# A hybrid decoder layer on one core: recursion heads in two contiguous halves, output weights split later, 112 places per expert dealt over 16 groups of rows

## The chip, the cores and the metric

The kernel runs as one program on one core of a Trainium2 chip. The metric is the time of one execution in device microseconds. Of the kernel before there are three runs, 2958.97 to 2961.05 us, with a median of 2959.9 us. The profile of it is of a further execution, which took 2961.59 us; its trace spans 2959.8 us, and TensorE's mean granted clock in it is 0.96 of full speed.

The engines are called PE (TensorE), ACT (ScalarE), DVE (VectorE), POOL (GpSimd) and SP (SyncE, which here does little but issue transfers); a q behind the name (SPq) is the sequencer of that engine, which issues its transfers.

## The reference

One layer with 2048 tokens of 1024 numbers. Eight heads run a recursion over time, eight others an attention with forgetting; their outputs go through one output projection, and a mixture of 64 small experts follows, two per token.

```python
h = rms_norm(x, norm_mix_w)
p = h @ w_in
y_rw = rwkv7_mixer(p[..., :RW_COLS], ...)   # 8 heads of 64: S_t = S_{t-1} diag(w_t) + (S_{t-1} a_t) b_t^T + v_t k_t^T; y_t = S_t r_t
y_fox = fox_mixer(p[..., RW_COLS:], ...)    # 8 heads of 64: causal softmax attention, logits shifted by a running sum of log f
x = x + concatenate([y_rw, y_fox]) @ w_out
h = rms_norm(x, norm_ffn_w)
# hierarchical_moe: the best of 8 groups, in it the best 2 of 8 experts; gates from two softmaxes
y = sum over a token's 2 experts of gate * ((silu(h @ w_gate[e]) * (h @ w_up[e])) @ w_down[e])   # 1024 -> 512 -> 1024
x = x + y
```

With the reference's inputs the router gives an expert 64 tokens on average (4096 over 64 experts) and at most 101. Experts 0, 1 and 2 get 63, 52 and 30, the last two 50 and 79.

## The kernel before

**Stages.** The tokens are worked in 16 tiles (i) of 128. The projection of the recursion's heads fills the time to about 600 us, the attention's projection follows to about 850 us. Then attention and recursion run side by side to about 1430 us, the output projection, the norm, the router and the expert tables (`mix`) to about 1735 us, and the experts (`moe`) to the end. In every stage the order of the instructions on PE, ACT, DVE and POOL is written by a planner (`Lanes`): each piece of work is a generator which yields the engine and a modelled cost before its instructions, or the name of an event it waits for; `lanes.mark(name, delay)` sets an event. SP's transfers go into the program at the moment at which the planner reaches them, and SP issues them in that order; the planner gives them no cost.

**Recursion (`chain`).** Each tile is handled in 4 chunks (c) of 32 tokens. `gram2` and `gram3` have computed the chunk's small matrices before and written them to a tensor in DRAM per tile, `pkd`; the blocks of inverses lie in another, `TTd`. `load(i)` fetches a tile from there: AM (lines 1340 to 1342), TTb (line 1346), and for each of two kinds of heads (`e`, which lie in different halves of the partitions) the operands UV and SW (line 1357), YW (lines 1359 and 1362) and the decay `dec` (line 1364). Head h is here 2q + e: kind 0 holds the even heads and kind 1 the odd ones, so that in DRAM each kind is every other block of 64 columns. That is why line 1357 issues one transfer per chunk: 4 + 8 per kind, 24 per tile. A tile has 39 such loads, and `outputs` writes its result to `yd` in 8 transfers. A chunk makes `us` from UV on PE, copies it back into UV (ACT, line 1400), then makes the new state and the outputs Y; line 1380 is the first product of a tile with TTb.

**Output weights (`out_open`).** The two halves of `w_out` are loaded into `wst` (line 245, on SP) and each split into two fp16 parts: ACT makes the high part `wo` (line 255), DVE the low one (line 259). The first half's eight pieces are spread between the attention's work from the moment at which `out_open` starts.

**Tables (`mix`, `moe_table`).** For every token the router computes its two experts, its place in each (how many tokens chose it before), and the gate. POOL writes (token, gate) by an indirect transfer (line 1767) into row `place * 64 + expert` of one of two tables in DRAM, `tab[q]`. `moe_table` (line 1921) loads the first SL = 104 places of all experts into `tb`, place on partition: the first table by one transfer on POOL, the second by one on ACT. DVE then makes the index `idx` as the smaller of both (line 2008) and the gate as their sum. A place that no token took has an index beyond the last token, and a gather or a scatter skips it. Experts with more than SL tokens would get a second pass in a loop behind the stage, which with these inputs runs no time.

**Experts (`experts`).** Per expert: POOL gathers the token rows (line 2088, 4 KB each), PE transposes them (line 2104), the weights (gate, up, down; 2 MB each) come over SP into staging buffers `st` and are split into fp16 parts by ACT (line 1969) and DVE (line 1973), PE multiplies with gate and up (lines 2146 to 2148), `h` is made, transposed by PE in eight steps (line 2178) and copied to HT by ACT (line 2181), PE multiplies with down (lines 2139 to 2141), ACT scales by the gate (line 2196), and POOL adds the rows to the output by an indirect transfer (line 2202). In every product the places of the expert are the stationary side and 512 columns of weights stream. The staging buffers are dealt out by a list that is written by hand; from about the 33rd expert on all loads share four of them. In the planner a load costs 5.83 and a gather or a scatter 1.18 us of one common transfer queue ("Q").

Of the kernel before, what the change touches and what calls it, by code (L numbers as in the profile page):

```python
# [8 lines left out]
F32 = mybir.dt.float32  # L9
# [17 lines left out]
NG = 4  # L27
E = 64
DE = 512
SL = 104  # L30
NB = -(-T // SL)
CDEC = 0.5 * math.exp(-0.5)
WS = 64.0
# [69 lines left out]
class Kern:  # L103
# [453 lines left out]
    def rwkv_front(self):  # L557
# [8 lines left out]
        with ExitStack() as es:  # L566
# [223 lines left out]
            def gram2(i):  # L790

                s = St[i]
                A2, R2, BK = s["A2"], s["R2"], s["BK"]
                s["g1"] = g1 = smp.tile([128, 8, 2, 32], F32, name="g1", tag="sm")
                s["g2"] = g2 = smp.tile([128, 8, 2, 32], F32, name="g2", tag="sm")
                for h in range(8):
                    q, e = divmod(h, 2)
                    for c in range(4):
                        t = slice(32 * c, 32 * c + 32)
                        nc.tensor.matmul(g1[t, h], A2[:, e, q, t], BK[:, :, q, t], start=True, stop=True)  # L800
                for h in range(8):
                    q, e = divmod(h, 2)
                    for m in range(2):
                        for c in range(4):
                            t = slice(32 * c, 32 * c + 32)
                            nc.tensor.matmul(g2[t, h, m], BK[:, m, q, t], R2[:, e, q, t], start=True, stop=True)

            def gram3(i):
                s = St[i]
                g, j = divmod(i, 4)  # L810
                pk, g1, g2 = s["pk"], s["g1"], s["g2"]
                L = wk.tile([128, 8, 32], F32, name="L", tag="s0")
                ml = self.mlow[:, 0:1].to_broadcast([128, 8, 32])
                TT(L, g1[:, :, 0], ml)
                TT(s["AM"][:, :, 0:32], g1[:, :, 1], ml)
                for m, o in ((0, self.PK_QB), (1, self.PK_QK)):
                    TT(pk[:, o:o + 256].rearrange("p (e q t) -> p q e t", e=2, q=4),
                       g2[:, :, m].rearrange("p (q e) t -> p q e t", e=2),
                       self.mup[:, 0:1, None, :].to_broadcast([128, 4, 2, 32]))
# [489 lines left out]
    def chain(self, lanes, step_at, uwp, usp, yp):  # L1309
# [10 lines left out]
            yield "P", 0.9  # L1320
            nc.gpsimd.memset(t, 0.0)
        for s in range(2):
            t = self.pw.tile([128, 4, 8, 64], F32, name=f"UV{s}", tag=("l2", "l3")[s])
            yield "P", 1.8
            nc.gpsimd.memset(t, 0.0)
            UVs.append(t)
            t = (ch, self.pw)[s].tile([128, 32, 64], F32, name=f"SW{s}", tag=("SW", "h3")[s])
            yield "P", 1.9
            for e in range(2):
                r = slice(64 - 64 * e, 128 - 64 * e)  # L1330
                nc.gpsimd.tensor_scalar(t[r].rearrange("p (c e) d -> p c e d", e=2)[:, :, e],
                                        self.id32[r, None, r].to_broadcast([64, 16, 64]), 1.0, 0.0,
                                        op0=OP.mult, op1=OP.add)
            SWs.append(t.rearrange("p (c h) d -> p c h d", h=8))

        def load(i):
            s, pkd = St[i], self.pkd[i]
            g, j = divmod(i, 4)
            am, ma = AM.rearrange("p (q e) c -> p q e c", e=2), pkd[:, 0:768].rearrange("p (q e c) -> p q e c", q=4, e=2)
            nc.sync.dma_start(am[:, :, 0, 32:128], ma[:, :, 0])  # L1340
            nc.sync.dma_start(am[:, :, 1, 0:64], ma[:, :, 1, 32:96])
            nc.sync.dma_start(am[:, :, 1, 96:128], ma[:, :, 1, 0:32])
            for c in range(4):
                t = slice(32 * c, 32 * c + 32)
                o = (j * 4 + c) * 8
                nc.sync.dma_start(TTb[t, :, t], self.TTd[g][o:o + 8].rearrange("h (k i) -> k h i", k=32))
            ct = lambda o, n: pkd[:, o:o + n].rearrange("(c t) f -> t c f", c=4)
            s["YW"] = YW = ch.tile([128, 4, 2, 4, 32], F32, name="YW", bufs=2)
            s["dec"] = dec = ch.tile([128, 4, 4], F32, name="dec", bufs=2)
            for e in range(2):  # L1350
                u, st = 64 * e, slice(64 - 64 * e, 128 - 64 * e)
                hd = lambda x: x.rearrange("t c (q e d) -> t c q e d", e=2, d=64)[:, :, :, e]
                own = lambda x, r: x[r].rearrange("t c (q e) d -> t c q e d", e=2)[:, :, :, e]
                for x, m, o in ((UVs[i % 2], 1, self.PK_V), (SWs[i % 2], 0, self.PK_B), (SWs[i % 2], 1, self.PK_K)):
                    r = slice(u + 32 * m, u + 32 * m + 32)
                    for c in range(4):
                        nc.sync.dma_start(own(x, r)[:, c], hd(ct(o, 512))[:, c])
                for m, o in ((0, self.PK_QB), (1, self.PK_QK)):
                    nc.sync.dma_start(YW[u + 32 * m:u + 32 * m + 32, :, e].rearrange("p c q t -> p c (q t)"),
                                      ct(o + 128 * e, 128))  # L1360
                r = slice(u, u + 64)
                nc.sync.dma_start(YW[st, :, e].rearrange("p c q t -> p c (q t)"),
                                  pkd[r, self.PK_R:self.PK_R + 512].rearrange("p (c f) -> p c f", c=4))
                nc.sync.dma_start(dec[st].rearrange("p q c -> p (q c)"), pkd[r, self.PK_DEC:self.PK_DEC + 16])

        def prep(i):

# [18 lines left out]
        def chunk(i, c):  # L1386
# [1 line left out]
            yield f"t{step_at[8 * i + 2 * c]}"  # L1388
            yield "us"
            yield "T", 0.6  # L1390
            uv = UV[:, c].rearrange("p (q e) d -> p e q d", e=2)
            U = usp.tile([128, 4, 64], F32, name="us")
            for h in range(8):
                q, e = divmod(h, 2)
                nc.tensor.matmul(U[64 * e:64 * e + 32, q], UW[:, h, 32 * c:32 * c + 32], UV[:, c, h],
                                 start=True, stop=True)
            for e in range(2):
                yield "A", 0.32
                r = slice(64 * e, 64 * e + 32)
                nc.scalar.activation(uv[r, e], U[r], AF.Copy)  # L1400
            lanes.give("us")
            if c == 0:
                yield "Y"
# [1 line left out]
            if (i, c) != (NT - 1, 3):  # L1405
                yield "us"
                yield "T", 0.5
                S = usp.tile([128, 4, 64], F32, name="us")
                for h in range(8):
                    q, e = divmod(h, 2)  # L1410
                    nc.tensor.matmul(S[64 - 64 * e:128 - 64 * e, q], SW[:, c, h], UV[:, c, h], start=True, stop=True)
            lanes.start("y", outputs(i, c, UV))
            if (i, c) != (NT - 1, 3):
                nxt = UVs[i % 2][:, c + 1] if c < 3 else UVs[(i + 1) % 2][:, 0]
                nxt = nxt.rearrange("p (q e) d -> p e q d", e=2)
# [7 lines left out]
        def outputs(i, c, UV):  # L1423
            s = St[i]
            yield "T", 0.33
            for h in range(8):
                q, e = divmod(h, 2)
                r = 64 * e + 32 * (q % 2)
                nc.tensor.matmul(s["Y"][r:r + 32, c, q // 2], s["YW"][:, c, e, q], UV[:, c, h], start=True, stop=True)
            if c == 3:  # L1430
                yield "A", 0.48
                y = ch.tile([128, 4, 2, 64], F32, name="y", bufs=2)
                nc.scalar.activation(y, s["Y"], AF.Copy)
                yd = self.yd[i].rearrange("(c t) (p m e d) -> t m e c p d", c=4, p=2, m=2, e=2)
                for e in range(2):
                    for m in range(2):
                        r = 64 * e + 32 * m
                        for q in range(2):
                            nc.sync.dma_start(yd[:, m, e, :, q], y[r:r + 32, :, q])
                lanes.give("Y")  # L1440
                lanes.mark(f"tile{i}")

# [15 lines left out]
    def out_open(self):  # L1458
# [4 lines left out]
        wo = self.eo[0].tile([128, 2, KB, 512], F16, name="wo", tag="wo")  # L1463
        self.wo = [[wo[:, 0], wo[:, 1]]]
        split = self.split_block([w_out[:, :512]], None)
        yield from split.steps(*self.wo[0])
        yield "last"
        split = self.split_block([w_out[:, 512:]], None)
# [814 lines left out]
```

## Time and profile before

| | |
|---|---|
| median of 3 runs | 2959.9 us (2958.97 to 2961.05) |
| profiled execution, its span | 2961.59 us, 2959.8 us |
| PE busy | 2590.1 us (88%) |
| DVE busy | 2382.3 us (80%) |
| ACT busy | 1754.1 us (59%) |
| POOL busy | 814.1 us (28%) |
| transfers | 645.47 MB, mean 218 GB/s |

The profile divides the span into 40 equal slices of 74 us and gives the busy share of each engine per slice in tenths. PE's share of 88% is a mean over stages with different limits: it says little about what ends last in a stage. That is read from the waits, which name for each stretch of idle time the instruction that ended it, and from the timelines, in which each row has its start in us, its duration in us, the engine, the line of the kernel, the operation with its tiles, and in brackets the idle time before it with what ended it. In a window's row the busy time of PE, PE's weight loads, DVE, ACT and POOL stand in this order, each with its number of instructions, then PE's granted clock, the mean busy share of the 16 DMA engines and the GB/s that they moved.

### The profile page before, as it was taken

The page shows a single profiled execution, that of the slowest core. Times are in us where ns is not written, and L with a number is a line of the kernel's source. Part 1 is how long each engine was busy: PE and PEld are TensorE (multiplying, and loading weights), DVE is VectorE, ACT ScalarE, POOL GpSimd, SP SyncE. Part 2 cuts the span into 40 slices and gives each one's busy share as a digit, 9 for nine tenths or more (in the row PEclk, how much of TensorE's full clock was granted, in tenths as well). Part 3 has the DMA queues.
Part 4 walks back from the last instruction along what each step waited for, and adds up shares of the span by engine and source line. Part 5 has one row for each costly group of instructions (what it writes and reads, how often), then busy time and mean ns, then how long its engine had stood idle before and what let it go on. Part 6 is the DMA issues. An engine that isn't in the chain of part 4 may idle for free. (4 is left out here: it accounts for less than half of the span.)

```text
span 2959.8 us, 53150 instructions
## 1 busy us (share of the span) xinstructions
PE 2590.1 (88%) x20309; PEld 1442.4 (49%) x20309; DVE 2382.3 (80%) x4278; ACT 1754.1 (59%) x2470; POOL 814.1 (28%) x729
## 2 busy tenths in 40 slices
PE   4997888799998999989888859999999989999897
PEld 2554445345444555444344435555555555555554
DVE  6788898863565787868989879888889888888886
ACT  5544434422243555546344448888888778787786
POOL 2212111223033545435545431222221111111111
PEclk8999999899999999989998979999999999999999
DMA  5343434433244544432465369999999999999996
GB/s 175 126 160 110 139 136 151 154 115 91 91 122 105 124 94 120 90 89 76 155 225 170 136 221 349 361 361 349 359 346 360 337 357 359 356 357 363 361 364 210
DMA packets 313678, 645.47 MB, mean 218 GB/s; under 512 B 183850, under 2 KB 229152, under 8 KB 288077
## 3 DMA queue, kind: packets, MB, share of 16 engines
q1 hardware_dynamic: 292584, 603.71, 58.5%
q0 software_dynamic: 20720, 38.29, 5.3%
q8 instruction: 160, 2.62, 0.4%
q14 instruction: 97, 0.79, 0.1%
q10 hardware_dynamic: 117, 0.05, 0.0%
HBM read 539.24 MB, written 109.06 MB: 219 GB/s over the span
## 5 line engine op out<-in xcount | busy, mean ns | idle before, releaser
L2202 POOL DMA_INDIRECT out_dram<-o,idx x64 | 130.3, 2035 | 785.6 <-ACT o L2196 780.1
L1973 DVE SCALAR_TENSOR_TENSOR wh<-st,wh 128x1024 f16<-128x1024 f32 x224 | 269.3, 1222 | 57.2 <-ACT wh L1969 57.2
L1242 POOL TENSOR_TENSOR acc<-acc,P 128x128 f32<-128x128 f32 (+6 forms) x288 | 234.2, 833 | 186.5 <-ACT P L1205 171.1
L1973 DVE SCALAR_TENSOR_TENSOR h<-st,h 128x1024 f16<-128x1024 f32 x240 | 278.3, 1226 | 0.8 <-ACT h L1969 0.8
L1205 ACT ACTIVATE P<-st,biasT 128x512 f32<-128x512 f32 (+3 forms) x320 | 184.5, 620 | 155.8 <-PE st L1195 67.8
L1969 ACT ACTIVATE wh<-st 128x1024 f16<-128x1024 f32 x222 | 221.6, 1048 | 79.3 <-DMA st<-in_exp_w_gate_dram 41.9
L1969 ACT ACTIVATE h<-st 128x1024 f16<-128x1024 f32 x240 | 243.8, 1049 | 38.9 <-PE pd L2141 27.9
L2147 PE MATMUL gu<-wh,XT 128*104 128x512 f16 x512 | 194.6, 380 | 49.0 <-DVE wh L1973 49.0
L2139 PE MATMUL pd<-h,HT 128*104 128x512 f16 x504 | 192.1, 381 | 30.0 <-ACT HT L2181 30.0
L2148 PEld LDWEIGHTS <-XT 128*104 128x104 f16 x1024 | 129.5, 126 | 170.3 <-issue 91.2
L2146 PE MATMUL gu<-wh,XT 128*104 128x512 f16 x512 | 195.3, 381 | 4.4 <-ACT wh L1969 4.4
L1163 DVE TENSOR_REDUCE mx<-na 128x1 f32<-128x512 f32 (+3 forms) x296 | 171.4, 604 | 32.2 <-PE na L1075 21.5
L2148 PE MATMUL gu<-wh,XT 128*104 128x512 f16 x512 | 194.8, 380 | 0.1
L279 PE MATMUL mm<-rwh,hT 128*128 128x512 f16 (+1 forms) x512 | 185.1, 361 | 10.9 <-DVE pk L654 8.1
L2140 PE MATMUL pd<-h,HT 128*104 128x512 f16 x504 | 191.0, 379 | 0.6 <-DVE h L1973 0.6
L2141 PE MATMUL pd<-h,HT 128*104 128x512 f16 x504 | 191.0, 379 | 0.0
L280 PE MATMUL mm<-rwl,hT 128*128 128x512 f16 (+1 forms) x512 | 184.3, 360 | 2.8 <-DVE rwl L259 2.7
L281 PE MATMUL mm<-rwh,hT 128*128 128x512 f16 (+1 forms) x512 | 184.0, 359 | 0.9 <-ACT hT L635 0.9
L2147 PEld LDWEIGHTS <-XT 128*104 128x104 f16 x1024 | 130.2, 127 | 82.5 <-issue 6.7
L2146 PEld LDWEIGHTS <-XT 128*104 128x104 f16 x1024 | 129.9, 127 | 76.5 <-issue 0.4
L1973 DVE SCALAR_TENSOR_TENSOR xt<-st,xt 128x1024 f16<-128x1024 f32 x120 | 146.6, 1222 | 19.5 <-ACT xt L1969 19.5
L1227 PE MATMUL O<-P,Vp 128*64 128x512 f32 (+3 forms) x640 | 159.6, 558 | 2.9 <-ACT P L1205 2.9
(446 smaller groups left out, 6820.1 us busy)
## 6 DMA issues: line engine op xcount, KB each, us to landing
st<-in_exp_w_up_dram SPq DMA_DIRECT2D x55, 2048.0 KB
st<-in_exp_w_down_dram SPq DMA_DIRECT2D x54, 2048.0 KB
st<-in_exp_w_gate_dram SPq DMA_DIRECT2D x51, 2048.0 KB
pkd<-pk SPq DMA_DIRECT2D x16, 1740.0 KB
xt<-in_x_dram SPq DMA_DIRECT2D x32, 512.0 KB
wst<-in_exp_w_gate_dram SPq DMA_DIRECT2D x32, 512.0 KB
d<-mp SPq DMA_DIRECT2D x48, 224.0 KB
hTd<-hT SPq DMA_DIRECT2D x16, 512.0 KB
```

Source lines behind the costliest of these rows:

```text
L279: nc.tensor.matmul(ps, xh(k), wh(k), start=(k == 0), stop=False)
L280: nc.tensor.matmul(ps, xh(k), wl(k), start=False, stop=False)
L1205: nc.scalar.activation(P[:, :n], ps[:, :n], AF.Exp, bias=self.bias[:, g, kb, 2 * hp + s:2 * hp + s + 1])
L1242: e.tensor_tensor(acc, acc, P[:, lo:hi], op=OP.add)
L1969: self.nc.scalar.activation(h[:, 0], st, AF.Copy, scale=WS)
L1973: self.nc.vector.scalar_tensor_tensor(h[:, 1], st, WS, h[:, 0], op0=OP.mult, op1=OP.subtract)
L2139: nc.tensor.matmul(pd[s], HT[:, 0, q], h[:, 0, c], start=(q == 0), stop=False)
L2140: nc.tensor.matmul(pd[s], HT[:, 0, q], h[:, 1, c], start=False, stop=False)
L2141: nc.tensor.matmul(pd[s], HT[:, 1, q], h[:, 0, c], start=False, stop=(q == 3))
L2146: nc.tensor.matmul(p, XT[:, 0, x], h[:, 0, k], start=(x == 0), stop=False)
L2147: nc.tensor.matmul(p, XT[:, 0, x], h[:, 1, k], start=False, stop=False)
L2148: nc.tensor.matmul(p, XT[:, 1, x], h[:, 0, k], start=False, stop=(x == KB - 1))
```

## The change

**Kinds of heads.** The two kinds are now heads 0 to 3 and heads 4 to 7. `gram2` and `gram3` put the matrices of a kind side by side, `load` fetches a kind as one block of 256 columns for all four chunks, and the products take the same heads under other indices. UV and SW take 6 transfers per tile instead of 24; YW's R part and `dec` take 8 instead of 4, as the two head pairs of a kind are fetched apart; `yd` takes 4 instead of 8. Per tile SP issues 25 + 4 transfers instead of 39 + 8. The bytes are the same.

**Output weights.** Before the first half's split `out_open` sets an event with a delay of 24 us of the planner's time and waits for it.

**Places.** SL is 112. The table is loaded in 14 transfers, all on ACT: group j of 16 places goes to the partitions j, j + 7, j + 14, ..., so that place 16j + i lies on partition 7i + j, and successive places lie 7 partitions apart. XG, `o`, the transposes' outputs and the stationary sides grow to 112 places with it.

```diff
-SL = 104
+SL = 112
@@ gram2
-    nc.tensor.matmul(g2[t, h, m], BK[:, m, q, t], R2[:, e, q, t], start=True, stop=True)
+    nc.tensor.matmul(g2[t, q // 2 * 4 + 2 * e + q % 2, m], BK[:, m, q, t], R2[:, e, q, t], start=True, stop=True)
@@ load
-                    for c in range(4):
-                        nc.sync.dma_start(own(x, r)[:, c], hd(ct(o, 512))[:, c])
+                    nc.sync.dma_start(x[r, :, e].rearrange("p c q d -> p c (q d)"), ct(o + 256 * e, 256))
...
-                r = slice(u, u + 64)
-                nc.sync.dma_start(YW[st, :, e].rearrange("p c q t -> p c (q t)"),
-                                  pkd[r, self.PK_R:self.PK_R + 512].rearrange("p (c f) -> p c f", c=4))
-                nc.sync.dma_start(dec[st].rearrange("p q c -> p (q c)"), pkd[r, self.PK_DEC:self.PK_DEC + 16])
+                for m in range(2):
+                    r = slice(64 * m, 64 * m + 64)
+                    R = pkd[r, self.PK_R:self.PK_R + 512].rearrange("p (c f) -> p c f", c=4)
+                    nc.sync.dma_start(YW[st, :, e, 2 * m:2 * m + 2].rearrange("p c q t -> p c (q t)"),
+                                      R[:, :, 64 * e:64 * e + 64])
+                    o = self.PK_DEC + 8 * e
+                    nc.sync.dma_start(dec[st].rearrange("p (q m) c -> p m q c", m=2)[:, m],
+                                      pkd[r, o:o + 8].rearrange("p (q c) -> p q c", q=2))
@@ outputs
-                    for m in range(2):
                         r = 64 * e + 32 * m
-                        for q in range(2):
-                            nc.sync.dma_start(yd[:, m, e, :, q], y[r:r + 32, :, q])
+                        nc.sync.dma_start(yd[:, m, e], y[r:r + 32].rearrange("t c p d -> t c (p d)"))
@@ out_open
         split = self.split_block([w_out[:, :512]], None)
+        self.lanes.mark("wo0", 24)
+        yield "wo0"
         yield from split.steps(*self.wo[0])
@@ moe_table
-        for q, queue in enumerate((self.nc.gpsimd, self.nc.scalar)):
-            queue.dma_start(self.tb[:, q], self.tab[q].rearrange("(s e) c -> s e c", e=E)[0:SL])
+        for j in range(SL // 16):
+            for q in range(2):
+                src = self.tab[q][j * 16 * E:(j + 1) * 16 * E].rearrange("(i e) c -> i e c", e=E)
+                self.nc.scalar.dma_start(self.tb[j::SL // 16, q], src)
```

On SP, this is the second kind's half of a tile's loads with the first loads of `w_out` behind it, in the kernel before (pkd_111 is the tile's tensor in DRAM, UV_10254 and SW_10272 the buffers of the even tiles).

```order
L1357 DMA UV_10254<-pkd_111 32x4x64 x4
L1357 DMA SW_10272<-pkd_111 32x4x64 x8
L1359 DMA YW<-pkd_111 32x4x128 x2
L1362 DMA YW<-pkd_111 64x4x128
L1364 DMA dec<-pkd_111 64x16
L245 DMA wst<-in_w_out_dram 128x2x512 x4
```

The same place after the change:

```order
L1353 DMA UV_10254<-pkd_111 32x4x256
L1353 DMA SW_10272<-pkd_111 32x4x256 x2
L1355 DMA YW<-pkd_111 32x4x128 x2
L1361 DMA YW<-pkd_111 64x4x64
L1364 DMA dec<-pkd_111 64x2x4
L1361 DMA YW<-pkd_111 64x4x64
L1364 DMA dec<-pkd_111 64x2x4
L245 DMA wst<-in_w_out_dram 128x2x512 x4
```

Twelve transfers of UV and SW have become three, two of R and `dec` four; the loads of `w_out` stand behind the same tile as before.

On ACT, this is the place where the first pieces of the output weights stood in the kernel before (P, `Os` and `den` belong to the attention).

```order
L1257 ACTIVATE Os<-O 128x512
L1205 ACTIVATE P<-st,biasT 128x512 x2
L255 ACTIVATE wo<-wst 128x512
L1270 ACTIVATE den<-st 128x512
L255 ACTIVATE wo<-wst 128x512
L1205 ACTIVATE P<-st,biasT 128x384 x2
```

After the change no `wo` stands there; the first one comes some 30 rows later on ACT, behind the next tile's chunk (`us` and UV are the recursion's):

```order
L1400 ACTIVATE UV_10254<-us 32x256
L1204 ACTIVATE P<-st,biasT 128x512
L1400 ACTIVATE UV_10254<-us 32x256
L255 ACTIVATE wo<-wst 128x512
L1102 ACTIVATE QX_7175<-na 2x1024
```

So the first `wo` has moved behind a part of the attention and the recursion that stood after it, and its load has not.

On ACT at the end of `mix`, with tab_71 and tab_72 the two tables, the kernel before has one of the table's two loads (POOL has the other, behind its last scatter into the tables):

```order
L1969 ACTIVATE h_17460<-wst 128x1024 x2
L1776 ACTIVATE eg,sg<-lgs,ng 128x8
L1777 ACTIVATE zz<-zz 128x2
L1921 DMA tb<-tab_72 104x128
L1969 ACTIVATE wh<-st_17467 128x1024 x3
```

After the change the first two of fourteen, which alternate between the tables:

```order
L1975 ACTIVATE h_17172<-wst 128x1024 x2
L1778 ACTIVATE eg,sg<-lgs,ng 128x8
L1779 ACTIVATE zz<-zz 128x2
L1927 DMA tb<-tab_71 16x128
L1927 DMA tb<-tab_72 16x128
```

All the table's loads now stand on ACT, ahead of its first work on an expert's weights, and POOL has none. In the experts' stage the order of the instructions is the same on every engine.

## Rows read from the trace of the kernel before

**Rows 1.** Page, part 2: busy tenths of 16 DMA engines, 40 slices.
```profile
DMA  5343434433244544432465369999999999999996
```

**Rows 2.** Waits of TensorE, 840:1430: operation, releaser, total us, times, longest.
```profile
PE st L1194 <- ACT den L1270: 14.1, 1, 14.1
PE na L1380 <- DMA TTb<-TTd: 11.1, 2, 9.1
PE Y L1429 <- DMA YW<-pkd: 3.8, 2, 2.7
```

**Rows 3.** ScalarE's timeline, 1286:1306: start, duration, instruction, [idle before].
```profile
1304.03 0.63 ACT L255 ACTIVATE wo<-wst 128x512 f16<-128x512 f32 x1 [15.98 <-DMA wst<-in_w_out_dram]
```

**Rows 4.** Windows: busy us by engine, then PEclk, DMA share, GB/s.
```profile
1300.00:1320.00 20.00, 14.44 (x147) 7.90 (x147) 12.84 (x25) 11.26 (x24) 7.11 (x12) 0.71 0.38 127
```

**Rows 5.** SP queue's timeline, 855 to 900 us.
```profile
857.63 4.24 SPq L1357 DMA_DIRECT2D SW<-pkd  x8
861.97 0.85 SPq L1359 DMA_DIRECT2D YW<-pkd  x2
862.87 0.62 SPq L1362 DMA_DIRECT2D YW<-pkd  x1
863.53 0.61 SPq L1364 DMA_DIRECT2D dec<-pkd  x1
864.19 2.01 SPq L1357 DMA_DIRECT2D UV<-pkd  x4
...
872.29 0.60 SPq L1057 DMA_DIRECT2D KN<-KAd  x1
```

**Rows 6.** POOL's timeline: scatters of experts 1, 2, 28, 62, 63.
```profile
1796.40 2.21 POOL L2202 DMA_INDIRECT out_dram<-o,idx  x1 [11.09 <-ACT o L2196]
...
1814.83 2.40 POOL L2202 DMA_INDIRECT out_dram<-o,idx  x1 [12.13 <-ACT o L2196]
...
2285.58 1.87 POOL L2202 DMA_INDIRECT out_dram<-o,idx  x1 [11.90 <-ACT o L2196]
...
2938.60 2.18 POOL L2202 DMA_INDIRECT out_dram<-o,idx  x1 [21.36 <-ACT o L2196]
2946.21 1.59 POOL L2202 DMA_INDIRECT out_dram<-o,idx  x1 [5.43 <-DMA out_dram<-o,idx]
```

**Rows 7.** Waits of ScalarE, 2300 to 2900 us.
```profile
ACT xt L1969 <- DMA st<-in_exp_w_up_dram: 48.1, 24, 3.3
ACT wh L1969 <- DMA st<-in_exp_w_gate_dram: 41.9, 27, 3.5
```

**Rows 8.** Waits of TensorE, 1800 to 2300 us.
```profile
PE pd L2139 <- ACT HT L2181: 29.5, 19, 1.6
```

**Rows 9.** Timeline of all engines, start of the experts, 1735:1750.5.
```profile
1736.32 0.61 ACTq L1921 DMA_DIRECT2D tb<-tab  x1
1738.40 0.22 DVE L2008 TENSOR_TENSOR idx<-tb 104x64 int32<-104x64 f32 x1
...
1749.91 0.88 PE L2104 MATMUL pt<-id,xg 104*128 104x104 f16 x8 [17.52 <-DMA xg<-h2d,idx]
```

**Rows 10.** Line 472's DMA (16 rows): ns min/median/max, start us.
```profile
L472 SPq DMA_DIRECT2D cTd<-cT x1: 338/338/338, 786.0 to 786.0; - x1
```

**Rows 11.** TensorE's timeline: eight transposes of one expert.
```profile
2933.91 0.53 PE L2178 MATMUL pt<-id,h 104*128 104x104 f16 x8
```

**Rows 12.** Lines 2178 and 2181, 1800:2900: ns min/median/max.
```profile
L2178 PE MATMUL pt<-id,h x472: 207/209/220, 1804.8 to 2886.2; 104*128 104x104 f16 x158
...
L2181 ACT ACTIVATE HT<-pt x59: 839/846/864, 1806.0 to 2886.7; 128x832 f16<-128x832 f16 x59
```

**Rows 13.** Windows: gathers alone, weights alone, last scatter alone.
```profile
1748.00:1749.00 1.00, 0.00 (x0) 0.00 (x0) 0.00 (x0) 0.00 (x0) 0.00 (x0) 0.50 0.48 152
1908.00:1911.00 3.00, 3.00 (x22) 1.90 (x21) 0.94 (x2) 2.62 (x3) 1.43 (x1) 1.00 1.01 431
2950.00:2951.00 1.00, 0.00 (x0) 0.00 (x0) 0.00 (x0) 0.00 (x0) 0.00 (x0) 0.50 0.68 123
```

More of the change, by code (lines that the diff above doesn't have):

```diff
@@ L816, in gram3 @@
                 for m, o in ((0, self.PK_QB), (1, self.PK_QK)):
-                    TT(pk[:, o:o + 256].rearrange("p (e q t) -> p q e t", e=2, q=4),
-                       g2[:, :, m].rearrange("p (q e) t -> p q e t", e=2),
-                       self.mup[:, 0:1, None, :].to_broadcast([128, 4, 2, 32]))
+                    TT(pk[:, o:o + 256].rearrange("p (h t) -> p h t", h=8), g2[:, :, m],
+                       self.mup[:, 0:1].to_broadcast([128, 8, 32]))
                 nc.vector.tensor_reduce(pk[:, self.PK_BON:self.PK_BON + 8], h8(s["r"]), axis=AX.X, op=OP.add)
@@ L1322, in chain @@
         for s in range(2):
-            t = self.pw.tile([128, 4, 8, 64], F32, name=f"UV{s}", tag=("l2", "l3")[s])
+            t = self.pw.tile([128, 4, 2, 4, 64], F32, name=f"UV{s}", tag=("l2", "l3")[s])
             yield "P", 1.8
@@ L1330, in chain @@
                 r = slice(64 - 64 * e, 128 - 64 * e)
-                nc.gpsimd.tensor_scalar(t[r].rearrange("p (c e) d -> p c e d", e=2)[:, :, e],
-                                        self.id32[r, None, r].to_broadcast([64, 16, 64]), 1.0, 0.0,
+                nc.gpsimd.tensor_scalar(t[r].rearrange("p (c e q) d -> p c e q d", e=2, q=4)[:, :, e],
+                                        self.id32[r, None, None, r].to_broadcast([64, 4, 4, 64]), 1.0, 0.0,
                                         op0=OP.mult, op1=OP.add)
-            SWs.append(t.rearrange("p (c h) d -> p c h d", h=8))
+            SWs.append(t.rearrange("p (c e q) d -> p c e q d", e=2, q=4))
         def load(i):
@@ L1338, in load @@
             g, j = divmod(i, 4)
[L1339 to L1342, printed above, removed]
+            ma = pkd[:, 0:768].rearrange("p (h c) -> p h c", h=8)
+            nc.sync.dma_start(AM[:, 0:4, 32:128], ma[:, 0:4])
+            nc.sync.dma_start(AM[:, 4:8, 0:64], ma[:, 4:8, 32:96])
+            nc.sync.dma_start(AM[:, 4:8, 96:128], ma[:, 4:8, 0:32])
             for c in range(4):
@@ L1351, in load @@
                 u, st = 64 * e, slice(64 - 64 * e, 128 - 64 * e)
-                hd = lambda x: x.rearrange("t c (q e d) -> t c q e d", e=2, d=64)[:, :, :, e]
-                own = lambda x, r: x[r].rearrange("t c (q e) d -> t c q e d", e=2)[:, :, :, e]
                 for x, m, o in ((UVs[i % 2], 1, self.PK_V), (SWs[i % 2], 0, self.PK_B), (SWs[i % 2], 1, self.PK_K)):
                     r = slice(u + 32 * m, u + 32 * m + 32)
-                    for c in range(4):
-                        nc.sync.dma_start(own(x, r)[:, c], hd(ct(o, 512))[:, c])
+                    nc.sync.dma_start(x[r, :, e].rearrange("p c q d -> p c (q d)"), ct(o + 256 * e, 256))
                 for m, o in ((0, self.PK_QB), (1, self.PK_QK)):
@@ L1390, in chunk @@
             yield "T", 0.6
-            uv = UV[:, c].rearrange("p (q e) d -> p e q d", e=2)
             U = usp.tile([128, 4, 64], F32, name="us")
[L1393 to L1396, printed above, removed]
+            for q in range(4):
+                for e in range(2):
+                    nc.tensor.matmul(U[64 * e:64 * e + 32, q], UW[:, 4 * e + q, 32 * c:32 * c + 32], UV[:, c, e, q],
+                                     start=True, stop=True)
             for e in range(2):
@@ L1399, in chunk @@
                 r = slice(64 * e, 64 * e + 32)
-                nc.scalar.activation(uv[r, e], U[r], AF.Copy)
+                nc.scalar.activation(UV[r, c, e], U[r], AF.Copy)
             lanes.give("us")
@@ L1408, in chunk @@
                 S = usp.tile([128, 4, 64], F32, name="us")
-                for h in range(8):
-                    q, e = divmod(h, 2)
-                    nc.tensor.matmul(S[64 - 64 * e:128 - 64 * e, q], SW[:, c, h], UV[:, c, h], start=True, stop=True)
+                for q in range(4):
+                    for e in range(2):
+                        nc.tensor.matmul(S[64 - 64 * e:128 - 64 * e, q], SW[:, c, e, q], UV[:, c, e, q], start=True,
+                                         stop=True)
             lanes.start("y", outputs(i, c, UV))
@@ L1414, in chunk @@
                 nxt = UVs[i % 2][:, c + 1] if c < 3 else UVs[(i + 1) % 2][:, 0]
-                nxt = nxt.rearrange("p (q e) d -> p e q d", e=2)
                 for e in range(2):
@@ L1425, in outputs @@
             yield "T", 0.33
[L1426 to L1429, printed above, removed]
+            for q in (0, 2, 1, 3):
+                for e in range(2):
+                    r = 64 * e + 32 * (q // 2)
+                    nc.tensor.matmul(s["Y"][r:r + 32, c, q % 2], s["YW"][:, c, e, q % 2 * 2 + q // 2],
+                                     UV[:, c, e, q], start=True, stop=True)
             if c == 3:
@@ L1433, in outputs @@
                 nc.scalar.activation(y, s["Y"], AF.Copy)
-                yd = self.yd[i].rearrange("(c t) (p m e d) -> t m e c p d", c=4, p=2, m=2, e=2)
+                yd = self.yd[i].rearrange("(c t) (e m f) -> t m e c f", c=4, m=2, e=2)
                 for e in range(2):
```

## The prediction

> **What bounds the kernel now.** I read the page's slices first, then what TensorE (PE) waits for in the stage of the serial recursion, then the start and the rhythm of the expert stage. The DMA row shows two programs in one: to slice 24 the transfers are half idle, from slice 25 on they are nearly full [rows 1]. In the first part a queue or an engine that stands still costs time. In the second both the stream of weights and the arithmetic can set the pace.
>
> In the recursion (840 to 1430 us) three waits of PE matter: 14.1 us once for a softmax denominator, twice for a block of inverses (TTb; 11.1 us, 9.1 of them at once), 3.8 us for YW [rows 2]. The first is not a matter of softmax. ScalarE (ACT), which has to copy the denominator, stood 15.98 us at an output weight whose load had not landed [rows 3]. Afterwards PE ran at a granted clock of 0.71 [rows 4]. The other two waits lie behind the SP queue, which issues one recursion tile's loads as a long line of small transfers [rows 5].
>
> The expert stage: an expert's scatter follows the one before by 18.43 us early on (1796.40, 1814.83); between 2285.58 and 2938.60 lie 34 intervals of 19.21 us on average [rows 6]. In the late part ACT waits for weights (48.1 + 41.9 us) [rows 7], in the early part PE waits for HT, a chain of arithmetic (29.5 us) [rows 8]. So the late part is bound by transfers, the early part is not.
>
> **Output weights split later.** The first of the eight conversions moves behind another tile's work on ACT; its load keeps its place in the SP queue. The 14.1 us go [rows 2]. PE's slower stretch goes with them: 14.44 us of work at 0.71 [rows 4] is at most 14.44 x 0.29 = 4.2 us too long; I take 2. Late next would be the following tile's loads, and these get shorter. Term: -16 (bounds -12 and -18).
>
> **Recursion heads in contiguous halves.** UV and SW take 6 transfers instead of 24, YW's R part and dec 8 instead of 4, yd 4 instead of 8. From SW at 857.63 to the first attention load (KN) at 872.29 SP needs 14.7 us. Afterwards, at the durations of the same rows: SW twice 1.0, YW 0.85, R and dec twice each 2.46, UV 0.5, then SW, YW, R and dec again: 9.2 us [rows 5]. Everything behind comes 5.5 us earlier, TTb too, for which PE waited 9.1 us: -5.5. The waits for YW in the next tile lie behind the same line, which shrinks once more: -3.8 [rows 2]. A faster clock after the shorter gap: -1, an estimate after rows 4. Two masked products on VectorE and the copies into UV change their shape, not their 256 elements: nothing. Later tiles gain nothing, as PE hardly waits there. Term: -10 (bounds -4, if TTb stays behind the big loads in front of it, and -15).
>
> **The table in 14 transfers.** Before, POOL and ACT each issue one; ACT's goes out at 1736.32, the indices are made at 1738.40, and PE then waits 17.52 us in all for the first gathered tokens: nothing covers this [rows 9]. Now ACT issues all 14. The trace shows no 16-row transfer on ACT. On SP one of 16 rows takes 0.34 [rows 10], ACT's own of 104 rows 0.61 [rows 9]; most small ones on SP lie at 0.43 to 0.5 (SW, YW, UV) [rows 5], and I take 0.43. The 13 after the first add 13 x 0.43 = 5.6. Term: +5.5 (bounds +4 and +8). [...]
>
> **112 places.** No expert gets more than 101 tokens (worked out from the reference's routing), so the overflow loop runs as little as before, and the token rows moved are the same. The products stream 512 columns of weights whatever the places. Eight transposes take 0.53, 0.21 of it the last one's length: a step of 0.046 for 104 columns, 0.0035 more for 112, times 24 = 0.08 us per expert. HT's copy grows by at most 8/104 of 0.85 = 0.065 [rows 11, 12]. So 0 to 0.15 per expert, on the path only where arithmetic sets the pace. Term: +3 for the 28 early experts at 0.1 (bounds 0, and +9.6 for all 64 at 0.15).
>
> **Rows dealt over 16 groups.** This is the largest term. The first three gathers carry 63, 52 and 30 tokens. With nothing else on the DMA engines, they keep 0.48 x 16 = 7.7 of them busy at 152 GB/s: 8 engines take everything. A row costs 4096 B / (152/7.7 GB/s) = 0.21 us. The last scatter (79 rows) holds 0.68 x 16 = 10.9 engines at 123 GB/s: about ten engines with 8 rows each, 0.36 us per row [rows 13]. Consecutive places thus lie on the first engines: for 64 tokens, the mean, 8 engines carry 8 x (0.21 + 0.36) = 4.6 us per expert on top of their share of three weight matrices, 6.29 MB at 431 GB/s [rows 13] = 14.6 us. Sum 19.2: just the rhythm of the late part. (As I read it, the early part lives on loads made ahead, until these are used up.) Dealt, every engine has 4 rows: 14.6 + 2.3 = 16.9, less than the arithmetic needs. The late part then falls to the early rhythm with its 0.1; as some waits will remain with 16.9 so near, I take 18.4: 34 x (19.21 - 18.4) = -27. Bounds: 0 (the first rival below), and -51 at 17.7, were HT, which hardly holds PE late, no limit.
>
> [...]
>
> **Ends.** The first gather has 4 rows per engine instead of 8: 4 x 0.21, -1. At the end the last scatter waits 5.43 us for the one before [rows 6]; their 50 and 79 rows take 4 and 5 per engine instead of 8: (4 + 3) x 0.36, -2.5 (bounds 0 and -4).
>
> **Sum.** -16 - 10 + 5.5 + 3 - 27 - 1 - 2.5 = -48. The profiled execution took 2961.6 (span 2959.8 and 1.8 around it), 1.7 above the median of 2959.9. So 2961.6 - 48 - 1.7 = 2912.
>
> **Rivals.**
> *The expert stage keeps its rhythm*: the rows are evened out anyway, or the late part hangs on its four staging buffers and the time from issue to landing. For it: the mean DMA share of the late slices is 0.9 or more [rows 1], which leaves little idle to win. Against: the start's rows and the match of 19.2. Without the -27: 2939.
> *It speeds up more*: with transfers no longer late the late part runs at 17.7, since HT holds PE only early [rows 8]. 51 instead of 27: 2888. Against: no reason that the late order is so much better.
> *The table is served one transfer at a time*, each from issue to landing, 2.1 us (1736.32 to 1738.40) [rows 9]: 14 x 2.1 - 2 = +27 in place of +5.5: 2934.
> *Work grows with the places* (the slower side): if an expert's cost on the path grew like its places, by 8/104 of 18.43 = 1.42 us, 64 experts would pay 91, and the -27 and +3 fall away: 2912 + 27 - 3 + 91 = 3027. The other terms give -24, so this mechanism decides from 24/64 = 0.38 us per expert on. Against: only transposes and copies have the places in their length [rows 11, 12].
> *The gains of the recursion are given back* by waits in the stage after it, and the rhythm stays: within 0.2% of before.
>
> **How the numbers follow.** A measurement of this kernel can tell about 0.2% (6 us) from no change. Forecast 0.48, rhythm kept 0.22, faster rhythm 0.13, serial table 0.06, growth with places 0.06, given back 0.05. Faster: 0.48 + 0.22 + 0.13 + 0.06 = 0.89; within 0.05; slower 0.06. The forecast's own range is 2897 to 2927; with the rhythm kept and the faster one at its edges, 2886 to 2942.
>
> **What would show it.** Recursion: no wait of ACT at wo, TTb's wait near 3.5 us, SP about 9 us from SW to the attention loads. Table: indices 4 to 8 us later after the last table scatter. Experts: late intervals near 18.4 and ACT's waits for weights under a third of what they were; in the first gathers and the last scatter all 16 engines busy, for half as long. Early intervals above 18.6 would speak for growth with places; late ones still at 19.2 would make the largest term wrong, and 17.7 too small.

## The result and the profile after

The changed kernel takes 2910.72 us (median of 4 runs, 2907.48 to 2912.27) against 2959.85 us (2958.97 to 2961.05), a ratio of 0.9831 with a 95% interval of 0.9818 to 0.9843: 49 us faster. The forecast was 2912. The profiled execution spans 2910.5 us, 49.3 less than before. Read at six points of the two timelines (the rows of before are in [rows 6, 9], those of after below; the last scatters into the tables, before and after, come first), the 49.3 us divide as follows.

```profile
1734.14 0.96 POOL L1767 DMA_INDIRECT tab<-ent,ri  x1 [0.31 <-issue]
...
1705.37 0.96 POOL L1769 DMA_INDIRECT tab<-ent,ri  x1 [0.30 <-issue]
```

| stretch | before | after | difference | forecast |
|---|---|---|---|---|
| start to last scatter into the tables | 1734.14 | 1705.37 | -28.8 | -26 |
| from there to the indices | 4.26 | 11.69 | +7.4 | +5.5 |
| indices to first transposes of an expert | 11.51 | 11.68 | +0.2 | -1 |
| to the scatter of expert 28 | 535.67 | 538.46 | +2.8 | +3 |
| 34 late intervals | 653.02 | 625.61 | -27.4 | -27 |
| scatter of expert 62 to the end | 21.2 | 17.7 | -3.5 | -2.5 |

In the recursion the row of the longest wait [rows 2] is gone; of the wait for TTb 4.3 us of 11.1 are left, and YW has no row. TensorE's waits, 840 to 1430 us, two of the first rows:

```profile
PE na L1381 <- DMA TTb<-TTd: 4.3, 1, 4.3
PE st L1265 <- POOL acc L1241: 2.8, 1, 2.8
```

The SP queue issues one tile's loads between the same two points as in [rows 5] in 10.2 us instead of 14.7, and on ACT the first output weight stands without any wait:

```profile
858.97 1.38 SPq L1353 DMA_DIRECT2D SW<-pkd  x2
...
869.15 0.60 SPq L1056 DMA_DIRECT2D KN<-KAd  x1
```

```profile
1299.42 0.63 ACT L255 ACTIVATE wo<-wst 128x512 f16<-128x512 f32 x1
```

At the start of the experts the fourteen table loads take ACT's queue 9.42 us, the indices follow, and TensorE's wait for the first gather has grown from 17.52 to 25.06 us [rows 9]:

```profile
1706.27 9.42 ACTq L1927 DMA_DIRECT2D tb<-tab  x14
...
1717.06 0.23 DVE L2014 TENSOR_TENSOR idx<-tb 112x64 int32<-112x64 f32 x1 [2.02 <-DMA tb<-tab]
...
1728.74 0.46 PE L2110 MATMUL pt<-id,xg 112*128 112x112 f16 x3 [25.06 <-DMA xg<-h2d,idx]
```

The scatters that answer to [rows 6]: early ones 18.54 us apart instead of 18.43, the 34 late intervals 18.40 on average (nearly all at 18.24 to 18.29; the last, a 23.20, is as long as before) instead of 19.21.

```profile
1775.30 2.05 POOL L2208 DMA_INDIRECT out_dram<-o,idx  x1 [11.23 <-ACT o L2202]
...
1793.84 2.28 POOL L2208 DMA_INDIRECT out_dram<-o,idx  x1 [12.23 <-ACT o L2202]
...
2267.20 1.78 POOL L2208 DMA_INDIRECT out_dram<-o,idx  x1 [11.92 <-ACT o L2202]
...
2892.81 2.06 POOL L2208 DMA_INDIRECT out_dram<-o,idx  x1 [21.46 <-ACT o L2202]
2898.62 1.46 POOL L2208 DMA_INDIRECT out_dram<-o,idx  x1 [3.74 <-DMA out_dram<-o,idx]
```

ACT's waits in the late part (2300 to 2900 us) no longer name a weight load [rows 7]; it now waits for TensorE, whose own longest row there is a wait of 32.0 us for weights that DVE splits. Early, TensorE waits for HT as before [rows 8], and HT's copy has grown from 846 to 917 ns, a transpose from 209 to 212 [rows 12].

```profile
ACT o L2202 <- PE pd L2147: 55.8, 32, 1.7
ACT h L2176 <- DVE sl L2171: 27.3, 33, 0.9
```

```profile
PE gu L2153 <- DVE wh L1979: 32.0, 90, 0.5
```

```profile
PE pd L2145 <- ACT HT L2187: 30.5, 21, 1.6
```

```profile
L2184 PE MATMUL pt<-id,h x472: 210/212/223, 1802.3 to 2858.4; 112*128 112x112 f16 x158
...
L2187 ACT ACTIVATE HT<-pt x59: 898/917/919, 1803.5 to 2858.9; 128x896 f16<-128x896 f16 x59
```

### The profile page after: what moved, and what is told of

The parts are those of the page before. It is cut to its first block, busy times and chain, and to the rows that moved or that the text cites. A ratio compares the mean times of both kernels' runs of the same rounds, so it can differ in the third digit from the quotient of the medians.

```text
span 2910.5 us, 52852 instructions
## 1 busy us (share of the span) xinstructions
PE 2578.2 (89%) x20309; PEld 1456.2 (50%) x20309; DVE 2389.0 (82%) x4277; ACT 1755.2 (60%) x2470; POOL 809.3 (28%) x728
## 5 line engine op out<-in xcount | busy, mean ns | idle before, releaser
L2208 POOL DMA_INDIRECT out_dram<-o,idx x64 | 123.5, 1930 | 775.3 <-ACT o L2202 771.6
L2153 PE MATMUL gu<-wh,XT 128*112 128x512 f16 x512 | 194.0, 379 | 38.8 <-DVE wh L1979 38.4
L2145 PE MATMUL pd<-h,HT 128*112 128x512 f16 x504 | 191.9, 381 | 30.5 <-ACT HT L2187 30.5
L2154 PEld LDWEIGHTS <-XT 128*112 128x112 f16 x1024 | 132.6, 130 | 145.9 <-issue 66.6
L1162 DVE TENSOR_REDUCE mx<-na 128x1 f32<-128x512 f32 (+3 forms) x296 | 171.2, 604 | 33.3 <-PE na L1074 22.9
L2152 PE MATMUL gu<-wh,XT 128*112 128x512 f16 x512 | 194.9, 381 | 0.0
L2154 PE MATMUL gu<-wh,XT 128*112 128x512 f16 x512 | 194.2, 379 | 0.0
L2146 PE MATMUL pd<-h,HT 128*112 128x512 f16 x504 | 191.0, 379 | 0.5 <-DVE h L1979 0.4
L2147 PE MATMUL pd<-h,HT 128*112 128x512 f16 x504 | 191.0, 379 | 0.0
L2153 PEld LDWEIGHTS <-XT 128*112 128x112 f16 x1024 | 133.4, 130 | 73.6 <-issue 0.2
L2152 PEld LDWEIGHTS <-XT 128*112 128x112 f16 x1024 | 133.0, 130 | 73.5
L279 PE MATMUL mm<-fwh,hT 128*128 128x512 f16 (+1 forms) x512 | 157.5, 330 | 1.6 <-ACT vt L370 1.6
```

What stands on the lines that cost most here:

```text
L279: nc.tensor.matmul(ps, xh(k), wh(k), start=(k == 0), stop=False)
L2145: nc.tensor.matmul(pd[s], HT[:, 0, q], h[:, 0, c], start=(q == 0), stop=False)
L2146: nc.tensor.matmul(pd[s], HT[:, 0, q], h[:, 1, c], start=False, stop=False)
L2147: nc.tensor.matmul(pd[s], HT[:, 1, q], h[:, 0, c], start=False, stop=(q == 3))
L2152: nc.tensor.matmul(p, XT[:, 0, x], h[:, 0, k], start=(x == 0), stop=False)
L2153: nc.tensor.matmul(p, XT[:, 0, x], h[:, 1, k], start=False, stop=False)
```

## The experiments

Each kernel was run beside the kernel before on the same chip; ratios are to it.

**The two edits of the recursion, one at a time.** The output weights alone, on the kernel before:

```diff
+        self.lanes.mark("wo0", 24)
+        yield "wo0"
         yield from split.steps(*self.wo[0])
```

> The kernel before with the delayed start of the output-weight split alone. Theory (the wait of 14.1 us and the slower clock behind it go): -16, 2944 us; ACT no longer waits for the first wo, TTb's waits of 11.1 us stay. Rival (the time is given back by the next late load or by the stage behind): within 4 us of 2960. If the two edits of the recursion share one cause, the queue of loads on SP, this one alone may give nearly all of the 28.8 us that the recursion and the mix lost together: 2931.

Measured: 2943.2 us (2940.36 to 2947.23), ratio 0.9951 (0.9934 to 0.9967), 16.3 us faster by the medians, as the theory had it; the 2931 of a single common cause did not come. The wait of 14.1 is gone, TTb's total stands unchanged:

```profile
PE na L1380 <- DMA TTb<-TTd: 11.1, 3, 8.4
```

In the trace, which is of the execution of 2940.36 us, the last scatter into the tables comes 20.4 us earlier.

The kinds of heads alone (104 places, two table loads, no delay of the output weights):

> The change's contiguous kinds of heads alone: 104 places, the table in two loads, the output weights split as early as before. Theory (two separate gains): TTb's 9.1 and YW's 3.8 us shrink, 10 to 13 us faster: 2947 to 2950; ACT still waits some 16 us for the first wo. Rival (one cause): with a shorter line on SP the load of w_out goes out earlier too, the wait at wo shrinks by the same 9 us or so, and this edit alone gives 20 or more: 2940 or less.

Measured: 2940.4 us (2936.84 to 2941.53), ratio 0.9933 (0.9916 to 0.9949), 19.1 us faster by the medians, the last table scatter 22.9 us earlier in the trace. Each edit alone gives most of the 28.8, and the two together 14 us less than the sum of both traces. The rival came in part: SP issues the load of `w_out` at 1277.87 instead of 1300.27, and ACT's wait for it falls from 15.98 to 7.80 us, TensorE's behind it from 14.1 to 6.0. The following rows are of this run: SP's queue, ACT's timeline and TensorE's waits (840 to 1430 us).

```profile
1277.87 2.13 SPq L245 DMA_DIRECT2D wst<-in_w_out_dram  x4
```

```profile
1281.67 0.63 ACT L255 ACTIVATE wo<-wst 128x512 f16<-128x512 f32 x1 [7.80 <-DMA wst<-in_w_out_dram]
```

```profile
PE st L1193 <- ACT den L1269: 6.0, 1, 6.0
PE na L1381 <- DMA TTb<-TTd: 5.2, 2, 4.4
```

So ACT's wait had two causes at once: the split stood early on ACT, and its load stood behind a long line on SP. Either edit removes part of the same wait.

How much of the 14 us this is can be read from two rows of ACT which stand on either side of the wait in each of the four kernels: the copies into UV of the 53rd and of the 55th of the recursion's 64 chunks. The kernel before, output weights alone, heads alone, both:

```profile
1282.65 0.76 ACT L1400 ACTIVATE UV<-us 32x256 f32<-32x256 f32 x2
1314.33 0.75 ACT L1400 ACTIVATE UV<-us 32x256 f32<-32x256 f32 x2
...
1278.66 0.76 ACT L1400 ACTIVATE UV<-us 32x256 f32<-32x256 f32 x2
1293.44 0.37 ACT L1400 ACTIVATE UV<-us 32x256 f32<-32x256 f32 x1
...
1268.46 0.76 ACT L1400 ACTIVATE UV<-us 32x256 f32<-32x256 f32 x2
1291.94 0.75 ACT L1400 ACTIVATE UV<-us 32x256 f32<-32x256 f32 x2
...
1269.00 0.76 ACT L1400 ACTIVATE UV<-us 32x256 f32<-32x256 f32 x2
1283.78 0.37 ACT L1400 ACTIVATE UV<-us 32x256 f32<-32x256 f32 x1
```

From the one to the other it is 31.7 us before, 14.8 with the output weights alone, 23.5 with the heads alone, and 14.8 with both. The overlap is therefore the 8.2 us that the heads alone take off this stretch. Of the rest, 4.0 us lie ahead of the stretch in the trace of the output weights alone, where that edit changes nothing: that much one execution differs from another.

**112 places without dealing.** In the changed kernel the table is loaded as before, place p on partition p:

```diff
-        for j in range(SL // 16):
...
+        for q, queue in enumerate((self.nc.gpsimd, self.nc.scalar)):
+            queue.dma_start(self.tb[:, q], self.tab[q].rearrange("(s e) c -> s e c", e=E)[0:SL])
```

> The changed kernel with the places of the table packed again (place p on partition p, two loads of 112 rows, as before), still 112 places. Theory (the largest number of rows on one DMA engine counts): 7 rows instead of 4 for an expert of 64 tokens, 14.6 + 7 x 0.57 = 18.6 us per expert in the late part instead of 18.27: +11, the ends +2, the table's loads -7.4: 2916. Rival A (112 places use all 16 engines, dealing adds nothing): late intervals stay at 18.27, 2903. Rival B (packing is all that counts): late intervals back at 19.2, +31 and +3 - 7.4: 2937.

Measured: 2936.85 us (2936.28 to 2939.14), ratio 0.9927 (0.9910 to 0.9943). My 2916 fell, rival B's 2937 came: the 34 late intervals are 19.42 us on average, and ACT waits 120 us for weights. Its scatters of experts 28, 48, 61 and 62:

```profile
2255.04 1.78 POOL L2204 DMA_INDIRECT out_dram<-o,idx  x1 [11.93 <-ACT o L2198]
...
2644.05 1.78 POOL L2204 DMA_INDIRECT out_dram<-o,idx  x1 [12.54 <-ACT o L2198]
...
2892.09 1.75 POOL L2204 DMA_INDIRECT out_dram<-o,idx  x1 [16.30 <-ACT o L2198]
2915.30 2.06 POOL L2204 DMA_INDIRECT out_dram<-o,idx  x1 [21.47 <-ACT o L2198]
```

ACT's waits, 2300 to 2880 us:

```profile
ACT xt L1971 <- DMA st<-in_exp_w_up_dram: 82.9, 30, 3.6
ACT wh L1971 <- DMA st<-in_exp_w_gate_dram: 28.3, 28, 1.7
ACT h L1971 <- DMA st<-in_exp_w_down_dram: 8.5, 22, 1.4
```

112 places as such give the late part nothing. By the counts, 64 packed tokens are at most seven rows for each of 16 groups of places, and eight for each of 13: seven cost no less than eight (19.42 us per late interval against 19.21).

**The dealt table in two transfers.** One on POOL and one on ACT, each reading DRAM in the dealt order:

```diff
-        for j in range(SL // 16):
...
+        for q, queue in enumerate((self.nc.gpsimd, self.nc.scalar)):
+            queue.dma_start(self.tb[:, q], self.tab[q][:SL * E].rearrange("(j i e) c -> i j (e c)", i=16, e=E))
```

> The changed kernel with the same dealt table, brought by two transfers (one on POOL, one on ACT) whose rows are read from DRAM in the dealt order, instead of fourteen on ACT. Theory (the fourteen loads lie on the path, 7.4 us longer than two): indices about 4.3 us after the last table scatter instead of 11.7, 2903; the experts' intervals are unchanged. Rival (nothing is won because the start of the experts waits for something else): 2911.

Measured: 2902.96 us (2901.10 to 2904.21), ratio 0.9811 (0.9795 to 0.9828), as expected: the indices come 4.57 us after the last table scatter, the late intervals are 18.38 on average. This kernel differs from the packed one only in the order of the rows, and is 33.9 us faster: that is what dealing is worth with 112 places.

**No rows at all.** In the kernel before, and then in the changed one, the index is the sum of the two tables:

```diff
-                nc.vector.tensor_tensor(idx, tb[:, 0, :, 0], tb[:, 1, :, 0], op=OP.min)
+                nc.vector.tensor_tensor(idx, tb[:, 0, :, 0], tb[:, 1, :, 0], op=OP.add)
```

> The kernel before, with the index made as the sum of the two tables instead of the smaller one: every index lies past the last token, so gathers and scatters move no row and the experts' part is left out of the output. All instructions and weight loads stay. Theory (the rows on the low DMA engines make the weights late): the late intervals fall from 19.21 to 18.2 or 18.3, and ACT's waits for weights in the late part from 99 us to under 20. Rival (four staging buffers and the time from issue to landing set the late rhythm): late intervals stay above 19.

Measured: 2921.26 us, ratio 0.9867 (0.9849 to 0.9885). The late intervals fall from 19.21 to 18.33 on average, and in ACT's waits (2300 to 2860 us) no weight load is left. Scatters of experts 28 and 62, then ACT's first two rows:

```profile
2280.80 1.86 POOL L2202 DMA_INDIRECT out_dram<-o,idx  x1 [11.84 <-ACT o L2196]
...
2904.02 2.18 POOL L2202 DMA_INDIRECT out_dram<-o,idx  x1 [21.37 <-ACT o L2196]
```

```profile
ACT o L2196 <- PE pd L2141: 52.4, 30, 1.8
ACT h L2170 <- DVE sl L2165: 24.2, 31, 0.9
```

> The changed kernel with all indices past the last token in the same way: no row is moved, the experts' part is left out of the output. Theory (with dealt rows arithmetic sets the pace): late intervals stay at 18.27 within 0.05; only the start and the end get shorter, by some 6 us each at most. Rival (the DMA engines, busy 99% of the late part, still set it): late intervals fall under 18.1.

Measured: 2904.2 us, ratio 0.9809 (0.9791 to 0.9827). The late intervals are 18.39 on average against 18.40 with rows:

```profile
2263.25 1.78 POOL L2208 DMA_INDIRECT out_dram<-o,idx  x1 [11.93 <-ACT o L2202]
...
2888.64 2.06 POOL L2208 DMA_INDIRECT out_dram<-o,idx  x1 [21.46 <-ACT o L2202]
```

Together these two settle where the largest term was: before, moving 64 token rows in and out per expert cost 30 us of the late part (34 x 0.88); dealt, it costs none. Neither buffers nor the weights alone set the rhythm of before. What bounds the late part after is arithmetic, at 18.25 us per expert, as its windows show, with rows (the changed kernel) and without:

```profile
2300.00:2850.00 550.00, 518.62 (x2892) 314.26 (x2891) 499.77 (x483) 455.89 (x512) 89.61 (x58) 1.00 1.00 372
...
2300.00:2850.00 550.00, 518.81 (x2895) 314.39 (x2893) 498.43 (x482) 457.28 (x513) 91.03 (x59) 1.00 0.90 342
```

Without rows the DMA engines are a tenth less busy, and nothing gets faster; TensorE is busy 94% of the time in both.

**Packed by turns.** For odd experts the two halves of the partitions are exchanged:

```diff
+        for q, queue in enumerate((self.nc.gpsimd, self.nc.scalar)):
+            src, h = self.tab[q].rearrange("(s e) c -> s e c", e=E), SL // 2
+            for to, of, v in ((0, 0, 0), (h, h, 0), (0, h, 1), (h, 0, 1)):
+                queue.dma_start(self.tb[to:to + h, q, v::2], src[of:of + h, v::2])
```

> 112 places, packed, but for every other expert the two halves of the partitions are exchanged, so that even experts start on partition 0 and odd ones on partition 56 (8 table loads). [...] Theory L (what counts is an engine's load over many experts): late intervals near 18.3. Theory X (what counts is how long one transfer holds its fullest engine): late intervals stay near 19.4. The time by L some 2905 to 2915, by X 2937 to 2947, the table's extra loads included.

Measured: 2920.06 us (2917.62 to 2925.83), ratio 0.9869 (0.9854 to 0.9884); the indices came 13.46 us after the last table scatter. The time lies between the ranges of both theories, and the late part splits in two. From expert 28 to 48 an interval is 18.28 us on average, in the packed run 19.45; from 48 to 61 it is 18.62, in the packed run 19.08. Scatters of experts 28, 48 and 61 of this run:

```profile
2265.86 1.77 POOL L2206 DMA_INDIRECT out_dram<-o,idx  x1 [11.92 <-ACT o L2200]
...
2631.46 1.77 POOL L2206 DMA_INDIRECT out_dram<-o,idx  x1 [12.04 <-ACT o L2200]
...
2873.57 1.74 POOL L2206 DMA_INDIRECT out_dram<-o,idx  x1 [16.27 <-ACT o L2200]
```

Both theories speak of engines, which no run shows one by one; what the runs differ in is the partitions. Theory X falls for the first twenty: within one transfer the rows stand on successive partitions as in the packed run, and the cost is gone (18.28 against 19.45). So how the rows of successive experts lie to each other made the difference there. For the second half the router's counts may give a part of the reason: experts 28 to 47 have 63 tokens on average, 48 to 61 have 79. The partitions behind either start are then full in every expert or nearly: if the partitions are taken in 16 groups of seven, which no run shows as such, the fullest carries 6.1 rows per expert in the first stretch and 7.0 in the second, worked out from the counts. ACT's waits for weights in this run are 1.5 us before 2631 and 36 us behind. But the packed run has the same 7.0 rows there and takes 19.08, not 18.62: the fullest group alone does not set the price, and what else does no run here shows.

**104 places, dealt over 13 groups, two transfers.**

```diff
-SL = 112
+SL = 104
...
+            queue.dma_start(self.tb[:, q], self.tab[q][:SL * E].rearrange("(j i e) c -> i j (e c)", i=13, e=E))
```

> The changed kernel with 104 places dealt over 13 groups of rows and the table brought by two transfers. Theory (5 rows on the fullest engine for an expert of 64 tokens are still covered, and 112 places cost 0.1 us per early expert): late intervals 18.25, early ones 18.44 instead of 18.55, 2900. [...]

Measured: 2904.07 us (2902.01 to 2908.20), ratio 0.9809 (0.9795 to 0.9822), no different from 112 places in two transfers. The early intervals are back at 18.44, and the stretch from the first scatter to the one of expert 28 is 2.7 us shorter than with 112 in two transfers (506.3 against 509.0). The late ones stand at 18.09 to 18.25, but for two near 18.5, until the intervals behind the 54th expert, two of which are 20.14 and 20.76: what the early part gains is lost there. So the theory held for experts of 64 tokens; it failed among the fuller ones (48 to 61, 79 tokens on average), with 6.6 rows on average in the fullest of 13 groups, worked out from the counts.

**The best version again.** The changed kernel and the one with two transfers, side by side:

> The changed kernel once more, beside the next one on the same chip: 2908 to 2913.

> The changed kernel with the dealt table in two transfers once more. Theory (the fourteen loads cost 7.4 us on the path): 6 to 9 us faster than the run before it, 2901 to 2905, and the intervals of the two do not overlap. Rival (the first comparison was scatter between runs): within 3 us of it.

Measured: 2910.38 us (2909.02 to 2911.29), ratio 0.9831 (0.9817 to 0.9844), and 2904.73 us (2899.93 to 2906.34), ratio 0.9805 (0.9791 to 0.9820). The runs do not overlap: two transfers are 5.7 us faster here, and 7.8 in the first comparison, which was not side by side. From the last table scatter to the indices it is 4.52 us instead of 11.72. This kernel beats both.

## Why the prediction was right, and where its working was not

**The sum** came out at -49.3 for a forecast of -48, each stretch of the table above within 3 us of its forecast. That it came so near is in part luck: the recursion's -2.8 and the ends' -1.0 beyond their forecasts met +1.9 at the table and +1.2 at the first gather.

**Recursion, -16 and -10; measured -28.8.** The mechanism held, and the two terms add up in the changed kernel: the stretch across the wait gives -16.9 (31.7 to 14.8 us), and what lies ahead of it -13.6 (1282.65 to 1269.00); a little is lost again behind it. The -10 is the term that came out too small, though how much is uncertain: the waits for TTb and YW gave 6.8 and 3.8 of it, and the kernel with the output weights alone, which has the old heads, is also 4.0 early there. What the working did not see is that the heads shorten the wait at `wo` by themselves, 8.2 us of it, since the shorter line on SP brings the load of `w_out` forward. "Its load keeps its place in the SP queue" was true of the order and said nothing of the time. The sum was not touched by it, as the -16 took the whole wait and the -10 no part of it.

**Table, +5.5; measured +7.4.** The mis-sized term is the duration of one transfer: I took 0.43 from SP's rows, and on ACT fourteen take 9.42 us, 0.67 each. ACT's own row of before, 0.61 for 104 rows [rows 9], would have given 13 x 0.61 = 7.9. The serial rival (2.1 us each) is refuted by the same row. Two in place of fourteen gave 5.7 to 7.8 us here: it was the spacing of their issue that cost, 0.67 us each.

**112 places, +3.** Right in size and place: 0.11 us per early interval, 2.8 to expert 28, with HT's copy 71 ns longer, and back at 18.44 in the run with 104. Growth with places by 0.38 us or more is refuted.

**Dealing, -27.** The mechanism, rows of tokens that make the weights late, is shown by the two runs without rows, and that it is their arrangement by the packed run, 33.9 us slower with the same loads and places. Two steps of the working failed. First, "14.6 + 8 x 0.57 = 19.2: just the rhythm" gives 18.6 for seven rows, where 19.42 was measured. The 14.6 was too small as well: without rows the engines are busy 0.90 of 18.25 us, which makes 16.4 us per expert for the weights (an estimate from that window), and 16.4 + 4.6 would be 21.0. The match with 19.2 was luck and no proof. Why seven rows in 16 groups cost as much as eight in 13 no run here settles. Second, "the late part falls to the early rhythm": the early rhythm (18.55) is held by HT, the late one is not and falls to 18.25, the limit of arithmetic that the run without rows shows. That the average is 18.40, as forecast, comes from the last interval, which is 23.2 in both kernels, and not from remaining waits: luck again. The faster rival (17.7) fails on the same limit; whether the transfers would have allowed 17.7 no run here shows.

The reading that packed places stay on the same engines fits what was seen, though no row here names an engine: taking turns alone brought 19.45 to 18.28 for the first twenty late experts, and the window at the start before shows eight engines' worth for three gathers [rows 13]. No run here shows it by itself. Nor does one show the rows of a single engine that the working and the expectations reckon with (8 packed and 4 dealt, 7 packed with 112 places, 5 dealt with 104). What the runs show in their place is the share of the 16 engines in one window of 1 us at the first gathers: 0.48 at 152 GB/s before [rows 13], 0.50 at 152 in the packed run with 112 places (1714:1715), and 1.01 at 193 in the changed kernel (1726:1727).

**Ends.** The last scatters gave -3.5, within the bounds: the last one waits 3.74 us for the one before instead of 5.43. The first gather, -1 in the sum, gave nothing, since the working took the price of a row as fixed. Two rows of the gathers' queue, each for one window of 1 us, with its packets, MB and share of the 16 engines; the first is of the kernel before (1748:1749 [rows 13]), the second of the changed kernel (1726:1727):

```profile
q0 software_dynamic: 74, 0.15, 47.6%
...
q0 software_dynamic: 133, 0.18, 92.3%
```

Dealt, the rows hold twice as many engines and move a fifth more: 0.34 us per 4 KB where 0.21 was taken, both estimates from such windows. Weights beside the rows are hardly the reason there: they hold 8% of the engines in that window. In the window ahead of it they hold 36%, and both together move 332 GB/s, but the first rows of before met weights as well (43% at 1746:1747).

```profile
1725.00:1726.00 1.00, 0.00 (x0) 0.00 (x0) 0.00 (x0) 0.00 (x0) 0.00 (x0) 0.50 1.06 332
```

Why a row costs more with all engines in use no run here shows.

## What to carry to other kernels

Where a stream of weights sets the pace, look at how the gathered rows lie over the partitions: here rows that are the same in number and bytes took 33.9 us more packed than dealt (2936.85 against 2902.96 us), by their arrangement alone. A new arrangement is best tried in the access pattern of one transfer, not in many small ones whose issue lies on the path: here two in place of fourteen brought the indices 4.5 to 4.6 us after the last table scatter instead of 11.7. When two edits shorten the same wait, one at the waiting instruction and one in the queue ahead of its load, the gains that they show alone must not be added: here 8.2 us were counted in both.

## What the runs showed of the hardware beyond that

Fourteen transfers of 16 rows on ACT's queue took 9.42 us, 0.67 each, about the same as one of 104 rows there (0.61): in these runs the number of transfers counted on that queue, not their size. Two transfers that read DRAM in permuted row order took hardly longer than two with plain order: the indices came 4.52 to 4.79 us after the last table scatter (three runs) against 4.22 to 4.28 (the kernel before and four runs). And a DMA share of 1.00 in the late part of the changed kernel did not mean that the transfers set its pace: at 0.90, without rows, it was no faster (late intervals of 18.40 and 18.39 us on average).
